# Splitting queries and keys into float32r parts at their projection instead of in the attention

## The chip, the cores and the metric

The kernel runs on one core of a Trainium2 chip. The metric is the device time in microseconds (us), the median of several runs. The engines are TensorE (PE, with its weight loads as PEld), VectorE (DVE), ScalarE (ACT), GpSimd (POOL) and SyncE (SP), which here issues the DMAs.

## The reference

One mixer layer on x of 2048 tokens and 1024 columns, all float32. A normalised input goes through one projection of 7168 columns; eight attention heads of 128 columns and four mLSTM heads use its parts; both results are gated, concatenated and projected back.

```python
h = rmsnorm(x, norm_g)
u = jnp.einsum("bsd,de->bse", h, w_in)                    # 1024 -> 7168
q_a, k_a, v_a, z_a, x_m, o_m, z_m = jnp.split(u, cuts, axis=-1)
for window, dilation in ((128, 1), (512, 4), (2048, 16)):
    o, l = dilated_window_attention(heads(q_a), heads(k_a), heads(v_a), window, dilation, slopes)
    ...
att = jnp.sum(wts[..., None] * jnp.stack(outs), axis=0) * silu(z_a)
...                                                       # conv, headwise linear, gates
hm = mlstm_chunkwise(q_m, k_m, v_m, log_i, log_f)         # then normalised per head, times silu(z_m)
x = x + jnp.einsum("bse,ed->bsd", concat([att, mls]), w_out)
return rmsnorm(x, final_g)
```

## The kernel before

**Precision.** A float32 operand is split into two float32r parts, hi (a rounded copy, ACT, L98) and lo (the rest, DVE, L99). A product is three matmuls: hi by hi, lo by hi, hi by lo.

**Projection (0 to about 1241 us).** There are 28 steps: two halves of the tokens (1024 each), and in each 14 steps for the kinds q, k, x, v, z, m, o, two steps each; the first are q0, q1, k0, k1. A step is seven products of a Strassen scheme, numbered 1 to 7; the operands of product m on the token side are the tiles h`m`h and h`m`l, on the weight side `whi` and `wlo`. Each product is 24 matmuls of 128x512 (L349) into PSUM tiles `pb` (two of them, for products 2, 1, 3 and 5; product 6 adds to the tile of 3) and `pa` (one, for 4; product 7 adds to it). `evac` adds them into the output tiles `o0` (one buffer) and `o1` (two) with ACT copies (L404) and DVE additions (L409, L411). After a step, `post` works on these tiles. For q and k it only stores them to `q_d` and `k_d` in DRAM; for the others it also applies a gate or the convolution.

**Background work.** `todo` is a list of generators, of which `run_post` takes one piece at each of four places in every product. Its first entry is `norm_later`: it normalises the second half's tokens in four blocks of two groups each. A group loads x into two `xc` tiles, squares them on ACT (L240, the output goes to `th` tiles), forms the inverse root on DVE (L243 to L94), scales (L247), transposes on PE (L252, four transposes of 128x128 at a time into the one PSUM tile `aux`), and copies with a factor on DVE (L255). Then each block makes seven Strassen operands (L262 on DVE, L265 on ACT; six of the seven combine or copy into `th` tiles) and stores them to `s_d` (L266). `scratch` gives tiles by tag: `xc` and `th` have two buffers each, and a tile is given out again only when everything that uses the earlier one is done.

**What sets the order.** Instructions are recorded in program order; a scheduler then fixes one order for each engine, and a piece of work that has to wait for a buffer of a tag stands behind the work that gives this buffer back.

**Attention and mLSTM (1241 to about 2109 us).** A head has 16 blocks, each twice (R=0, neighbouring keys; R=1, keys by residue of the token number), so 32 units; `attention` runs `qk` for one unit, `flip` for the unit two before, `pv` for the one three before, with the mLSTM and, later, the mLSTM half of the output projection (`early`) between them. `qk_split` (L617 on) prepares 512 tokens of a head: scaled hi and lo of q (ACT L620, DVE L621), both again in residue order (POOL L623, twice), and hi and lo of k (ACT L625, DVE L626). There are 32 such calls. `q_load` brings 256 KB, `k_load` 1 MB.

**Output projection (to 2217 us).** `early`, `att_tiles` and `load_wo` load raw 128x512 tiles (`wor`, `qh`) and split them into `me`, `we` and others (L98, L99); the matmuls are L1142 to L1144 and L1188 on.

Of the kernel before, what the change touches and what calls it, by code (L numbers as in the profile page):

```python
# [27 lines left out]
def kernel(  # L28
# [28 lines left out]
    q_d = dtile("q_d", [AH, 128, T])  # L57
    k_d = dtile("k_d", [AH, 128, T])
# [378 lines left out]

    def silu2(dst, th, src):
        nc.scalar.activation(th, src, AF.Tanh, scale=0.5)
        nc.vector.scalar_tensor_tensor(dst, th, 1.0, src, op0=ALU.add, op1=ALU.mult)  # L440

    def post(st, c):
# [14 lines left out]
        elif kind in "qkzm":  # L457
# [8 lines left out]
            dst = {"q": q_d, "k": k_d, "z": za_d}.get(kind)  # L466
            if kind == "m":
                for i in range(2):
                    nc.sync.dma_start(chunks(zm_d, e0 + i, hf * 8, 8), o[:, i, 3:].rearrange("p (c t) -> p c t", c=8))
            elif kind == "k":  # L470
                for i in range(2):
                    nc.sync.dma_start(residues(dst[e0 + i])[:, :, hf * 256:(hf + 1) * 256],
                                      o[:, i, 3:].rearrange("p (r q) -> p r q", r=4))
            else:
                nc.sync.dma_start(dst[e0:e0 + 2, :, tk].rearrange("e p t -> p e t"), o[:, :, 3:])
# [126 lines left out]

    def q_load(d, g):
# [11 lines left out]

    def qk_split(d, g):
        qr = d["qr", g] = by_r[-1]  # L617
        c = -1.0 / math.sqrt(128.0)
        hi, lo = qhi[:, g % 2], qt[:, g]
        nc.scalar.activation(hi, f(lo), AF.Copy, scale=c)  # L620
        nc.vector.scalar_tensor_tensor(lo, f(lo), c, f(hi), op0=ALU.mult, op1=ALU.subtract)  # L621
        for i, t in enumerate((hi, lo)):
            nc.gpsimd.tensor_copy(residues(qr[:, i, g % 2]), t.rearrange("p (j r) -> p r j", r=4))  # L623
        hi, lo = (residues(d[n])[:, :, g * 128:(g + 1) * 128] for n in ("kh", "k"))
        nc.scalar.activation(hi, f(lo), AF.Copy)  # L625
        nc.vector.tensor_tensor(lo, f(lo), f(hi), ALU.subtract)  # L626
# [39 lines left out]
    for i, (st, m) in enumerate(stream):  # L666
# [18 lines left out]
        if st == steps[-2] and m == ORDER[0]:  # L685
# [4 lines left out]
            qt = pre.tile([128, 4, 512], F32R, name="q")  # L690
            qhi = pre.tile([128, 2, 512], F32R, name="qh")
            first_load = k_load(pre, 0)
            for g in range(4):
                q_load(first_load, g)
# [27 lines left out]
    def qk(at, d, u):  # L722
        R, b = u
        g, r = b // 4, b % 4
        kh, kl, bl, st = d["kh"], d["k"], d["bl"], d["st"]
        ps = pq.tile([128, 512], F32, name="pq")
        if R:
# [3 lines left out]
            ks = lambda t: t[:, r * 512:r * 512 + n]  # L731
        else:
# [3 lines left out]
            ks = lambda t: t.rearrange("p (r b j) -> p b r j", r=4, b=16)[:, max(b - 1, 0):b + 1]  # L736
# [8 lines left out]
        qhr, qlr = (d["qr", g][:, i, g % 2] for i in range(2))  # L745
        qh, ql = (t[:, r * 128:(r + 1) * 128] for t in ((qhr, qlr) if R else (qhi[:, g % 2], qt[:, g])))
# [105 lines left out]
    def attention(at):  # L852
        qlag, slag = 0, 2
# [8 lines left out]
        for i in range(len(units) + 3):  # L862
            if i < len(units):
                h, u = units[i]
                if i == 0:
                    by_r.append(at.tile([128, 2, 2, 512], F32R, name="oL", bufs=2))
                    kh = at.tile([128, T], F32R, name="oR", bufs=2)
                    D_[0] = head_tiles(at, first_load)
                    D_[0]["kh"] = kh
                    qk_split(D_[0], 0)  # L870
                S_[i] = qk(at, D_[h], u)
# [7 lines left out]
            if i < len(units):  # L879
                h, (R, b) = units[i]  # L880
                if R and b % 4 == qlag and h + 1 < AH:
                    if b == qlag:
                        D_[h + 1] = k_load(at if h % 2 == 0 else pre, h + 1)
                    if b >= 4:
                        q_load(D_[h + 1], b // 4 - 1)
                if not R and b == qlag and h:
                    q_load(D_[h], 3)
# [174 lines left out]
    def raw_tile():  # L1062
        raws[0] += 1
        if raws[1] and raws[0] % 3 == 0:
            return pre.tile([128, 512], F32, name="qh")
        return woB.tile([128, 512], F32, name="wor", bufs=2)

    def att_tiles(b, i):
        if i == 0:
            pool, tag = ((pre, "q"), (ax[0], "qr"), (at, "kh"), (at, "k"))[mixes[0] % 4]  # L1070
            mixes[0] += 1
            MIX[b] = pool.tile([128, 2, 2, 4, 128], F32R, name=tag)
        t = MIX[b]
        raw = raw_tile().rearrange("p (e t) -> p e t", e=4)
        nc.sync.dma_start(raw, att_d[4 * i:4 * i + 4, :, b * 128:(b + 1) * 128].rearrange("e p t -> p e t"))
        split(t[:, i, 0], t[:, i, 1], raw)


    def load_wo(e):
# [3 lines left out]
        for n in range(2):  # L1083
            c = slice(n * 512, (n + 1) * 512)
            raw = raw_tile()
# [6 lines left out]
    def early():  # L1092
# [4 lines left out]
        def w_get(n, e):  # L1097
            raw["w", n, e] = woB.tile([128, 512], F32, name="wor", bufs=2)
            nc.sync.dma_start(raw["w", n, e], w_out[(KT + e) * 128:(KT + e + 1) * 128, n * 512:(n + 1) * 512])

        def w_split(n, e):
            t = W[n, e] = woB.tile([128, 2, 512], F32R, name=f"we{e}")
            split(t[:, 0], t[:, 1], raw.pop(("w", n, e)))
# [12 lines left out]

        seq = [(n, b) for n in range(2) for b in range(NB)]
        late = None
        w_get(0, 0)
        m_get(0, 0, 0)  # L1120
        w_split(0, 0)
        m_split(0, 0, 0)
        yield 0
        for e in range(1, 8):
            w_get(0, e)
            if e == 4:
                m_get(0, 0, 1)
                w_split(0, e)
                m_split(0, 0, 1)
            else:  # L1130
                w_split(0, e)
            if e % 2:
                yield 0
        for s, (n, b) in enumerate(seq):
# [4 lines left out]
            for e in range(8):  # L1139
# [9 lines left out]
                if swap:  # L1149
                    if e in (1, 2):  # L1150
                        w_get(1, e - 1)
# [3 lines left out]
                elif nxt:  # L1155
                    if e in (0, 3):
                        m_get(*nxt, e // 3)
                    if e == 4:
                        m_split(*nxt, 0)
# [3 lines left out]
            if swap:  # L1163
                for e in range(3, 8):
# [3 lines left out]
                    elif e < 8:  # L1168
                        m_get(*nxt, e - 6)
                    yield 0  # L1170
                m_split(*nxt, 0)
                m_split(*nxt, 1)
                yield 0
            elif nxt:
                m_split(*nxt, 1)
# [187 lines left out]
```

## Time and profile before

| | |
|---|---|
| Median of three runs | 2225.6 us (2224.17 to 2228.0) |
| The profiled execution, its own time | 2220.11 us |
| Its span (first to last instruction) | 2217.2 us |
| Mean granted TensorE clock | 0.988 |
| PE busy | 2126.7 us, 96% of the span |
| DVE, ACT, POOL busy | 1488.1, 942.8, 251.8 us |
| DMA read and written | 222.13 and 117.24 MB |

The page puts PE first: it is busy nearly always. The stages differ, though, so the table of windows, in which each row is a stage with every engine's busy time in it, is the one to read first. The list of waits says where an engine stood still and for what; the chain follows the work that ended last; the timeline gives single instructions with their start and duration. A matmul's busy time is longer than the spacing between two of them (0.39 us beside starts 0.23 us apart), since they overlap.

### The profile page before, as it was taken

What the parts mean: (1) busy time and instruction counts of PE and PEld (TensorE: products, weight loads), DVE (VectorE), ACT (ScalarE), POOL (GpSimd) and SP (SyncE); (2) the same over time, 40 slices, a digit from 0 to 9 for tenths busy, and PEclk for the clock granted to TensorE, in tenths of its full rate; (3) what the DMA queues carried; (4) which work ended last, traced back from release to release, by engine and by line L of the source; (5) the groups of instructions that cost most, each with busy time, mean ns of one, the idle gap of its engine ahead of it and who ended that gap; (6) DMA issues with size and microseconds to landing.
All of it is one profiled execution on the core that took longest, in us unless ns stands there. A gap on an engine that the chain in (4) does not pass through costs nothing.

```text
span 2217.2 us, 32676 instructions
## 1 busy us (share of the span) xinstructions
PE 2126.7 (96%) x11826; PEld 1788.0 (81%) x11826; DVE 1488.1 (67%) x3050; ACT 942.8 (43%) x1905; POOL 251.8 (11%) x221
## 2 busy tenths in 40 slices
PE   5999999999999999999999999999898999999998
PEld 4777888998878888787779888888887788777886
DVE  8887768556696558576666578868777644643654
ACT  6433333333383223334344555655555645532221
POOL 2200000000000000000000223343342221210000
PEclk9999999999999999999999999999999999999999
DMA  4256343432263333343324677776675664565442
GB/s 154 95 177 190 114 159 115 158 114 101 90 204 133 114 114 105 125 138 115 133 77 160 186 203 208 213 234 188 195 211 178 192 184 157 173 193 176 162 138 86
DMA packets 278896, 341.52 MB, mean 154 GB/s; under 512 B 22224, under 2 KB 194704, under 8 KB 276688
## 3 DMA queue, kind: packets, MB, share of 16 engines
q1 hardware_dynamic: 277872, 338.85, 48.2%
q8 instruction: 93, 1.52, 0.3%
q10 hardware_dynamic: 864, 0.59, 0.1%
q14 instruction: 67, 0.55, 0.1%
HBM read 222.13 MB, written 117.24 MB: 153 GB/s over the span
## 4 chain that ended last, share of the span: by engine, by line
PE 74%; DVE 9%; DMA 8%; issue 5%; ACT 3%; POOL 1%; SPq 0%; ACTq 0%; DVEq 0%; POOLq 0%
PE pb L349 31%; PE pa L349 12%; PE pm L780 3%; PE pu L997 2%; PE pt L762 2%; PE pu L985 2%; DMA wor<-mls_d 2%; DMA wor<-in_w_out 1%; DMA k<-k_d 1%; PE aux L500 1%; PE aux L510 1%; PE pq L748 1%; PE pq L750 1%; PE pq L749 1%; PE pu L982 1%
## 5 line engine op out<-in xcount | busy, mean ns | idle before, releaser
L98 ACT ACTIVATE whi<-ws 128x1024 fp32r<-128x1024 f32 x140 | 148.2, 1059 | 376.5 <-PE pb L349 209.4
L99 DVE TENSOR_TENSOR wlo<-ws,whi 128x1024 fp32r<-128x1024 f32 x140 | 171.8, 1227 | 81.3 <-ACT whi L98 80.4
L139 DVE TENSOR_TENSOR ws<-w,w 128x1024 f32<-128x1024 f32 x140 | 172.1, 1229 | 24.0 <-DMA w<-in_w_in 22.4
L754 ACT ACTIVATE s<-s,st 128x256 f32<-128x256 f32 (+3 forms) x256 | 134.9, 527 | 76.0 <-DVE st L752 68.8
L411 DVE TENSOR_TENSOR o<-pb,o 128x1024 f32<-128x1024 f32 x84 | 102.8, 1224 | 92.9 <-PE pb L349 91.9
L752 DVE CUSTOM_DVE_ANT_0 s<-pq,bl 128x256 f32<-128x256 f32 (+3 forms) x256 | 114.2, 448 | 43.3 <-PE pq L750 32.0
L612 POOL COPY bl<-bl 128x256 f32<-128x256 f32 x8 | 6.4, 796 | 1150.5 <-DMA q<-q_d 1111.3
L767 ACT ACTIVATE p<-pt 128x256 f32<-128x256 f32 (+1 forms) x192 | 81.3, 424 | 105.7 <-PE pt L762 104.6
L762 PE MATMUL pt<-sc,s 128*128 128x128 f32 x568 | 107.7, 279 | 7.1 <-ACT p L767 5.3
L98 ACT ACTIVATE whi<-w 128x1024 fp32r<-128x1024 f32 x56 | 59.2, 1057 | 125.2 <-PE pb L349 118.7
L1142 PE MATMUL pu<-we,me 128*128 128x512 f32 x256 | 106.6, 417 | 5.3 <-ACT me L98 4.4
L411 DVE TENSOR_TENSOR o<-pa,o 128x1024 f32<-128x1024 f32 x56 | 68.4, 1221 | 62.8 <-PE pa L349 62.8
L1143 PE MATMUL pu<-we,me 128*128 128x512 f32 x256 | 102.1, 399 | 2.9 <-DVE me L99 2.9
L1144 PE MATMUL pu<-we,me 128*128 128x512 f32 x256 | 101.2, 395 | 0.0
L780 PE MATMUL pm<-p,vc 128*128 128x128 f32 x640 | 96.3, 281 | 3.3 <-DVE p L765 1.7
L404 ACT ACTIVATE o<-pb 128x1024 f32<-128x1024 f32 x84 | 84.9, 1016 | 15.6 <-DVE o L411 9.8
L780 PEld LDWEIGHTS pm<-p,vc 128*128 128x128 f32 x640 | 84.0, 195 | 7.0 <-ACT p L767 3.5
L99 DVE TENSOR_TENSOR wlo<-w,whi 128x1024 fp32r<-128x1024 f32 x56 | 68.3, 1220 | 27.5 <-ACT whi L98 27.5
L762 PEld LDWEIGHTS pt<-sc,s 128*128 128x128 f32 x568 | 72.7, 143 | 17.3 <-ACT p L767 6.7
L99 DVE TENSOR_TENSOR me<-wor,me 128x512 fp32r<-128x512 f32 x64 | 48.4, 758 | 56.0 <-ACT me L98 55.9
L780 PE MATMUL pm<-p,vn 128*128 128x128 f32 x496 | 78.7, 279 | 5.1 <-ACT p L767 5.1
L997 PE MATMUL pu<-v,kw 128*128 128x257 f32 x240 | 71.6, 401 | 9.4 <-DVE C L1000 4.8
(592 smaller groups left out, 6565.9 us busy)
## 6 DMA issues: line engine op xcount, KB each, us to landing
w<-in_w_in SPq DMA_DIRECT2D x112, 512.0 KB
wor<-mls_d SPq DMA_DIRECT2D x64, 256.0 KB
q_d<-o SPq DMA_DIRECT2D x8, 1024.0 KB
k_d<-o SPq DMA_DIRECT2D x16, 512.0 KB
vm_d<-vm SPq DMA_DIRECT2D x32, 256.0 KB
xc_d<-xc SPq DMA_DIRECT2D x32, 256.0 KB
qm_d<-qm SPq DMA_DIRECT2D x32, 256.0 KB
v_d<-o SPq DMA_DIRECT2D x8, 1024.0 KB
```

The costliest lines, as they stand in the source:

```text
L98: nc.scalar.activation(hi, raw, AF.Copy)
L99: nc.vector.tensor_tensor(lo, raw, f(hi), ALU.subtract)
L139: eng.tensor_tensor(s, a, b, ALU.add if sign > 0 else ALU.subtract)
L349: nc.tensor.matmul(out, lhsT, rhs, start=start, stop=stop, skip_group_check=True)
L411: nc.vector.tensor_tensor(dst, ps, src, op)
L752: nc.vector.tensor_tensor_reduce(s[:, :n], ps[:, :n], bias, 1.0, 3e38, ALU.add, ALU.min, accum_out=st[:, col:col + 1])
L754: nc.scalar.activation(s[:, :n], s[:, :n], AF.Exp, bias=st[:, col:col + 1], scale=-1.0, accum_out=st[:, 16 + col:17 + col])
L762: nc.tensor.transpose(pp[:, i * 128:(i + 1) * 128], s[:, i * 128:(i + 1) * 128], ident)
L780: nc.tensor.matmul(od, v, p[:, j * 128:(j + 1) * 128], start=j == 0, stop=j == m - 1)
L997: nc.tensor.matmul(u[:, 0:257], kw[:, 2 * i + e, :], v[:, i], start=True, stop=True)
L1142: nc.tensor.matmul(acc, m[:, 0, j], w[:, 0], start=e == 0, stop=False)
L1143: nc.tensor.matmul(acc, m[:, 1, j], w[:, 0], start=False, stop=False)
```

## The change

In the projection, `post` no longer stores raw q and k. For every 128 x 512 part it calls `halves`, which makes hi (in an `xc` tile) and lo (in place in the output tile) and stores both; for q it also makes both again in residue order on ACT, in `th` tiles, and stores them. `q_d` grows fourfold and `k_d` twofold. In the attention `qk_split` is gone: `q_load` brings all four forms of 512 queries (1 MB) into one of two tiles, and the two parts of k are loaded by two DMAs of 1 MB (`k_load` and the one into `kh`); for the first eight blocks of head 0 hi of k comes as a quarter of that (`kh0`). In the output projection a raw tile of the mLSTM or attention result is loaded into the place of lo and split there, so that no `wor` tile is taken for it, and its load stands earlier.

```diff
+    def halves(kind, h, hf, g, raw):
+        hi = scratch("xc", 2).bitcast(F32R)
+        lo = raw.bitcast(F32R)
+        if kind == "q":
+            c = -1.0 / math.sqrt(128.0)
+            nc.scalar.activation(hi, raw, AF.Copy, scale=c)
+            nc.vector.scalar_tensor_tensor(lo, raw, c, f(hi), op0=ALU.mult, op1=ALU.subtract)
+            for n, t in enumerate((hi, lo)):
+                nc.sync.dma_start(q_d[h, 2 * hf + g][:, n], f(t))
+                rt = scratch("th", 2)
+                nc.scalar.activation(residues(rt), f(t).rearrange("p (j r) -> p r j", r=4), AF.Copy)
+                nc.sync.dma_start(q_d[h, 2 * hf + g][:, 2 + n], rt)
+                yield
+        else:
+            split(hi, lo, raw)
+            for n, t in enumerate((hi, lo)):
+                nc.sync.dma_start(residues(k_d[h, n])[:, 2 * g:2 * g + 2, hf * 256:(hf + 1) * 256],
+                                  f(t).rearrange("p (r q) -> p r q", r=2))
+            yield
...
+            elif kind == "z":
+                nc.sync.dma_start(za_d[e0:e0 + 2, :, tk].rearrange("e p t -> p e t"), o[:, :, 3:])
+            else:
                 for i in range(2):
+                    for g in range(2):
+                        yield from halves(kind, e0 + i, hf, g, o[:, i, 3 + g * 512:3 + (g + 1) * 512])
             yield
...
     def q_load(d, g):
-        nc.sync.dma_start(f(qt)[:, g], q_d[d["h"]][:, g * 512:(g + 1) * 512])
+        pool = (pre, ax[0] if ax else None)[g % 2]
+        d["q", g] = pool.tile([128, 4, 512], F32R, name="q") if pool else at.tile([128, 4, 512], F32R, name="oL", bufs=2)
+        nc.sync.dma_start(f(d["q", g]), q_d[d["h"], g])
...
-        nc.sync.dma_start(f(d["k"]), k_d[h])
+        nc.sync.dma_start(f(d["k"]), k_d[h, 1])
...
-    def qk_split(d, g):
...
                 if R and b == 11 and h + 1 < AH:
                     head_tiles(at, D_[h + 1])
-                    D_[h + 1]["kh"] = (at, ax[0])[h % 2].tile([128, T], F32R, name="kh")
-                if R and b % 4 == slag:
-                    if b < 12:
-                        qk_split(D_[h], b // 4 + 1)
-                    elif h + 1 < AH:
-                        qk_split(D_[h + 1], 0)
+                    kh = D_[h + 1]["kh"] = (at, ax[0])[h % 2].tile([128, T], F32R, name="kh")
+                    nc.sync.dma_start(f(kh), k_d[h + 1, 0])
+                if R and b % 4 == 1 and (h or b > 1):
+                    d, g = (D_[h], b // 4 + 1) if b < 12 else (D_.get(h + 1), 0)
+                    if d and g > (1 if h == 0 and d is D_[0] else -1):
+                        q_load(d, g)
...
+    def in_place(t):
+        split(t[:, 0], t[:, 1], f(t[:, 1]))
...
         def m_get(n, b, i):
-            raw["m", n, b, i] = woB.tile([128, 512], F32, name="wor", bufs=2)
-            nc.sync.dma_start(raw["m", n, b, i], mls_d[b, i])
-
-        def m_split(n, b, i):
             t = M[n, b, i] = woB.tile([128, 2, 4, 128], F32R, name="me", bufs=3)
-            split(t[:, 0], t[:, 1], raw.pop(("m", n, b, i)).rearrange("p (e t) -> p e t", e=4))
+            nc.sync.dma_start(f(t[:, 1]).rearrange("p e t -> p (e t)"), mls_d[b, i])
```

The number of matmuls does not change. How the change moves instructions is seen best in step q1, the second. On PE before, in products 7 of q1 and 2 of k0 (the numbers behind the names count tiles), two sets of `norm_later`'s transposes (L252, of four each) stand between the matmuls:

```order
L349 MATMUL pa_719<-h7h_493,whi_811 128x512
L349 MATMUL pa_719<-h7l_494,whi_811 128x512
L349 MATMUL pa_719<-h7h_493,wlo_812 128x512
L252 MATMUL aux_940<-sc_94,xc_903 128x128 x4
L349 MATMUL pa_719<-h7h_493,whi_811 128x512
L349 MATMUL pa_719<-h7l_494,whi_811 128x512
L349 MATMUL pa_719<-h7h_493,wlo_812 128x512
L349 MATMUL pb_1006<-h2h_194,whi_891 128x512
L252 MATMUL aux_953<-sc_94,xc_904 128x128 x4
L349 MATMUL pb_1006<-h2l_195,whi_891 128x512
```

On PE after, product 7 of q1 comes right behind product 3, and behind it stand the same two sets and all that follow, up to the last:

```order
L349 MATMUL pa_719<-h7h_493,wlo_812 128x512
L252 MATMUL aux_940<-sc_94,xc_903 128x128 x4
L252 MATMUL aux_953<-sc_94,xc_904 128x128 x4
L252 MATMUL aux_1084<-sc_94,xc_1040 128x128 x4
...
L252 MATMUL aux_1540<-sc_94,xc_1484 128x128 x4
L252 MATMUL aux_1590<-sc_94,xc_1553 128x128 x4
L252 MATMUL aux_1614<-sc_94,xc_1554 128x128 x4
L349 MATMUL pb_825<-h5h_606,whi_744 128x512
L349 MATMUL pb_825<-h5l_607,whi_744 128x512
```

Of the 64 transposes 56 (14 sets) now stand in one row without a product between them, and product 5 of q1 (`pb_825`) comes behind the last.

On ACT before, in the same step, the copy of product 1 out of PSUM (`o0_775<-pb_750`) stands among the rounding of weights (L98):

```order
L404 ACTIVATE o1_713<-pb_688 128x2x512
L98 ACTIVATE whi_744<-ws_746 128x1024
L98 ACTIVATE whi_779<-ws_781 128x1024
L404 ACTIVATE o0_775<-pb_750 128x2x512
L98 ACTIVATE whi_811<-ws_813 128x1024
L404 ACTIVATE o0_775<-pb_785 128x2x512
L98 ACTIVATE whi_891<-ws_893 128x1024
L240 ACTIVATE th_907,ss2_905<-xc_903 128x512
```

On ACT after, the same copy stands behind `norm_later`'s last pieces and behind `halves` of step q0 (L444 hi, L449 residue order; `o0_489` is the output tile of q0):

```order
L265 ACTIVATE th_1677<-gate_1619 128x512
L449 ACTIVATE th_1716<-xc_1712 128x512
...
L444 ACTIVATE xc_1846<-o1_341 128x512
L449 ACTIVATE th_1800<-o0_489 128x512
L404 ACTIVATE o0_775<-pb_750 128x2x512
L404 ACTIVATE o0_775<-pb_785 128x2x512
L449 ACTIVATE th_1827<-xc_1823 128x512
```

It was row 74 of ACT and is row 108: `o0` has one buffer, q0's `o0_489` is read until `th_1800`, and `halves` needs `xc` and `th` tiles, which come in turn behind all of `norm_later`. Product 5 takes the PSUM tile that this copy empties.

## Rows read from the trace of the kernel before

**Rows 1.** The page's head.
```profile
span 2217.2 us, 32676 instructions
```

**Rows 2.** Windows: start:end length, PE, PEld, DVE, ACT, POOL busy, PEclk, DMA share, GB/s.
```profile
106.00:235.00 129.00, 125.57 (x567) 99.56 (x566) 103.76 (x185) 42.61 (x62) 0.00 (x0) 1.00 0.57 181
235.00:1241.00 1006.00, 1005.94 (x5740) 849.04 (x5739) 669.06 (x720) 385.24 (x476) 0.65 (x1) 1.00 0.37 124
1241.00:1721.00 480.00, 444.46 (x2885) 395.91 (x2885) 365.64 (x1376) 280.65 (x850) 163.45 (x155) 0.96 0.71 209
1721.00:2109.00 388.00, 373.05 (x1886) 302.69 (x1886) 205.86 (x480) 158.65 (x383) 62.80 (x45) 1.00 0.56 177
2109.00:2217.00 108.00, 99.21 (x431) 80.46 (x429) 54.77 (x161) 20.34 (x53) 0.00 (x0) 0.97 0.33 110
```

**Rows 3.** The chain of waits, whole run: start us, us, what.
```profile
541.73 22.40 PE pb L349 x96
```

**Rows 4.** Timeline, PE in steps q1 and k1: start us, us, instruction, idle before.
```profile
106.42 0.39 PE L349 MATMUL pb<-h3h,wlo 128*128 128x512 f32 x1
106.65 0.39 PE L349 MATMUL pb<-h5h,whi 128*128 128x512 f32 x1
110.85 0.60 PE L252 MATMUL aux<-sc,xc 128*128 128x128 f32 x4
...
223.79 0.66 PE L252 MATMUL aux<-sc,xc 128*128 128x128 f32 x4
```

**Rows 5.** Timeline of one group of `norm_later`, all engines.
```profile
146.50 0.33 SPq L239 DMA_DIRECT2D xc<-in_x  x1
...
147.23 1.22 DVE L99 TENSOR_TENSOR wlo<-ws,whi 128x1024 fp32r<-128x1024 f32 x1
...
149.46 0.63 ACT L240 ACTIVATE th<-xc 128x512 f32<-128x512 f32 x1 [1.91 <-DMA xc<-in_x]
...
150.22 0.16 DVE L243 TENSOR_TENSOR ss<-ss 128x1 f32<-128x1 f32 x1 [0.51 <-ACT th L240]
```

**Rows 6.** Timeline of DVE in another group of `norm_later`.
```profile
172.79 0.16 DVE L243 TENSOR_TENSOR ss<-ss 128x1 f32<-128x1 f32 x1 [0.58 <-ACT th L240]
...
175.06 0.15 DVE L94 TENSOR_SCALAR rs_y<-rs_y 128x1 f32<-128x1 f32 x1
...
176.28 0.88 DVE L247 TENSOR_SCALAR xc<-xc,rs_y 128x512 f32<-128x512 f32 x2
177.51 0.69 DVE L255 TENSOR_TENSOR vm<-aux,ng 128x512 f32<-128x512 f32 x1 [0.34 <-PE aux L252]
```

**Rows 7.** The chain of waits from 100 to 240 us, the stores to `s_d`.
```profile
161.28 2.36 DMA s_d<-th
...
196.56 4.38 DMA s_d<-th
201.75 2.16 DMA s_d<-th
```

**Rows 8.** Waits in the attention and in `early`: who waits, for whom, us in total, times, longest.
```profile
PE pq L748 <- POOL oL L623: 1.5, 1, 1.5
...
ACT kh L625 <- DMA k<-k_d: 10.6, 4, 3.8
...
PE pu L1142 <- ACT me L98: 4.4, 3, 1.6
PE pu L1143 <- DVE me L99: 2.9, 6, 1.2
```

**Rows 9.** Windows, 7 us after the attention's start; columns as in Rows 2.
```profile
1245.00:1252.00 7.00, 6.23 (x29) 6.11 (x29) 3.69 (x17) 4.42 (x17) 3.73 (x4) 0.51 1.21 232
```

**Rows 10.** POOL's copies L623: their timeline beside DVE, and their sum in one window.
```profile
1573.86 1.10 POOL L623 CAST qr<-q 128x512 fp32r<-128x512 f32 x1 [0.76 <-DVE rs_y L86]
1574.04 0.94 DVE L92 TENSOR_TENSOR rs_t<-rs_t,sm 128x4 f32<-128x4 f32 x1
1575.83 0.16 DVE L92 TENSOR_TENSOR rs_t<-rs_t,sm 128x4 f32<-128x4 f32 x1
...
1241.00:1721.00 480.00, 65.09 (x240) 40.60 (x240) 0.00 (x0) 0.00 (x0) 48.05 (x43) 0.96 0.71 209
```

**Rows 11.** DMA: the queue's packets, MB, share of 16 engines; the issues for queries.
```profile
q1 hardware_dynamic: 277872, 338.85, 48.2%
...
q<-q_d SPq DMA_DIRECT2D x32, 256.0 KB
```

More of the change, by code (lines that the diff above doesn't have):

```diff
@@ L689 @@
             pre = prex.enter_context(tc.tile_pool(name="pre", bufs=1, side="right"))
-            qt = pre.tile([128, 4, 512], F32R, name="q")
-            qhi = pre.tile([128, 2, 512], F32R, name="qh")
+            kh0 = pre.tile([128, 1024], F32R, name="qh")
             first_load = k_load(pre, 0)
-            for g in range(4):
-                q_load(first_load, g)
+            q_load(first_load, 0)
+            nc.sync.dma_start(f(residues(kh0)), residues(k_d[0, 0])[:, :, 0:256])
     hx.close()
@@ L724, in qk @@
         g, r = b // 4, b % 4
-        kh, kl, bl, st = d["kh"], d["k"], d["bl"], d["st"]
+        kh, kl, bl, st = (residues(t) for t in (kh0 if d["h"] == 0 and b < 8 else d["kh"], d["k"])), None, d["bl"], d["st"]
+        kh, kl = kh
         ps = pq.tile([128, 512], F32, name="pq")
@@ L743, in keys @@
             return k
-        qhr, qlr = (d["qr", g][:, i, g % 2] for i in range(2))
-        qh, ql = (t[:, r * 128:(r + 1) * 128] for t in ((qhr, qlr) if R else (qhi[:, g % 2], qt[:, g])))
+        qh, ql = (d["q", g][:, 2 * R + i, r * 128:(r + 1) * 128] for i in range(2))
         w = max(n, 256)
@@ L865, in attention @@
                 if i == 0:
-                    by_r.append(at.tile([128, 2, 2, 512], F32R, name="oL", bufs=2))
+                    q_load(first_load, 1)
                     kh = at.tile([128, T], F32R, name="oR", bufs=2)
+                    nc.sync.dma_start(f(kh), k_d[0, 0])
                     D_[0] = head_tiles(at, first_load)
                     D_[0]["kh"] = kh
-                    qk_split(D_[0], 0)
+                h, u = units[i]
                 S_[i] = qk(at, D_[h], u)
@@ L1060, in mlstm, with att_get @@
             yield
[L1062 to L1066, printed above, removed]
+    def in_place(t):
+        split(t[:, 0], t[:, 1], f(t[:, 1]))
+    def att_get(b):
+        pool, tag = ((pre, "q"), (ax[0], "q"), (at, "kh"), (at, "k"))[b % 4]
+        MIX[b] = pool.tile([128, 2, 2, 4, 128], F32R, name=tag)
     def att_tiles(b, i):
         if i == 0:
[L1070 to L1076, printed above, removed]
+            att_get(b)
+        t = MIX[b][:, i]
+        nc.sync.dma_start(f(t[:, 1]), att_d[4 * i:4 * i + 4, :, b * 128:(b + 1) * 128].rearrange("e p t -> p e t"))
+        in_place(t)
     def load_wo(e):
@@ L1084, in load_wo @@
             c = slice(n * 512, (n + 1) * 512)
-            raw = raw_tile()
+            raw = woB.tile([128, 512], F32, name="wor", bufs=2)
             nc.sync.dma_start(raw, w_out[e * 128:(e + 1) * 128, c])
@@ L1115, in x_get, with w_split @@
             nc.sync.dma_start(raw["x", n, b], x[b * 128:(b + 1) * 128, n * 512:(n + 1) * 512])
+        def w_split(n, e):
+            t = woB.tile([128, 2, 512], F32R, name=f"we{e}")
+            split(t[:, 0], t[:, 1], W[n, e])
+            W[n, e] = t
         seq = [(n, b) for n in range(2) for b in range(NB)]
         late = None
[L1119 to L1132, printed above, removed]
+        for e in range(10):
+            if e >= 2:
+                w_split(0, e - 2)
+            if e < 8:
+                w_get(0, e)
+            if e % 4 == 3:
+                m_get(0, 0, e // 4)
                 yield 0
+        in_place(M[0, 0, 0])
+        in_place(M[0, 0, 1])
         for s, (n, b) in enumerate(seq):
@@ L1154, in early @@
                         w_get(1, e - 3)
[L1155 to L1159, printed above, removed]
+                if nxt:
+                    if e in (0, 2):
+                        m_get(*nxt, e // 2)
+                    if e in (4, 6):
+                        in_place(M[(*nxt, e // 2 - 2)])
             xr = raw.pop(("x", n, b))
@@ L1250 @@
     ax.append(ctx.enter_context(tc.tile_pool(name="ax", bufs=1)))
-    by_r.append(ax[0].tile([128, 2, 2, 512], F32R, name="qr"))
     with tc.tile_pool(name="mp", bufs=1) as mp:
```

61 lines of the change are left out of this document (13 added, 48 removed).

## The prediction

> **What bounds the kernel now.** I read the windows by stage first, then the chain, then the timeline of step q1, where the order changes, and last the waits of the attention. The windows show that the projection is TensorE from end to end: PE is busy 1005.94 of 1006 us there [rows 2], and one product after the other stands in the chain, four in 22.40 us, so 5.60 us each [rows 3]. Between 106 and 235 us `norm_later` runs beside it, and PE loses no more than 129 - 125.57 = 3.4 us [rows 2]. So whatever the change removes from DVE, ACT or POOL gains nothing in the projection, and whatever stops PE there is lost in full. In the attention (1241 to 1721) PE is idle for 480 - 444.46 = 35.5 us, and its mean granted clock is 0.96, which costs up to 0.04 x 480 = 19 us. From 1721 to 2109 it is idle for 15 us, at the end for 9 us [rows 2]. All that a lighter attention and output projection could give back is therefore 35.5 + 19 + 15 + 9 = 78 us at the very most.
>
> **Step q1: the new wait.** In the order of after, 14 sets of transposes of `norm_later` stand in one piece on PE, behind products 3 and 7 of q1 and ahead of product 5. Product 5 needs the PSUM tile that ACT's copy into `o0_775` empties; that copy now stands behind `th_1800`, the last of the residue copies that read `o0_489`; and these need `xc` and `th` tiles, which come behind all of `norm_later`. Queued behind the waiting matmul is everything that PE has left. Ahead of it on PE there are only transposes, so for this stretch the pace of `norm_later` by itself is the pace of the kernel. I sum it from the rows.
>
> Product 3 of q1 ends at 106.65 [rows 4]; with four sets of transposes (0.60 each, about 0.44 of it not overlapped) and product 7 (5.6) PE has done its matmuls at 106.65 + 5.6 + 4 x 0.44 = about 114. The first block's first group is transposed by about 109.
>
> One block, undisturbed, from the end of its first group's transposes to the same point of the next block:
> - its second group: load of x and two squares 150.22 - 146.50 = 3.7 [rows 5]; inverse root 175.06 + 0.15 - 172.79 = 2.4; scaling, two sets of transposes with the copy between them 2.6 (half of 0.88, then 0.60 + 0.69 + 0.60 and the hand-overs) [rows 4, 6]. Together 8.7.
> - its operands and the next block's first group: six operands go through two `th` tiles, the next squares need a `th` tile too, so three stores to `s_d` have to land one after the other. With r for one store and 0.7 for the operand ahead of it (the 0.69 of a DVE pass over 512 columns [rows 6]) this is 0.7 + 3 x (r + 0.7) + 0.8 for the squares [rows 5] + 2.4 + 2.6 = 8.6 + 3r.
>
> So a block takes 17.3 + 3r. The stores on the chain took 2.16 to 4.38 us [rows 7]. The queues are emptier in a stretch in which no weights are loaded, so I take r = 2.5 and get 25 us per block (24 with the shortest, 30.5 with the longest). The first block also has three operand builds of the weights left over on DVE, 3 x 1.22 [rows 5]. Its first group's point is 109, the fourth block's is 109 + 3.6 + 3 x 25 = 187.6, its second group is transposed at 196.3. Behind that come the last operands and the first halves of q, 14 `th` tiles up to `th_1800`, two at a time: six further trips of about 2.5 + 0.95 = 3.45, so 217. The copy (about 1 us) and the hand-over to PE bring product 5 to 219. PE thus stands from 114 to 219, 105 us, in which it does 14 sets of transposes (14 x 0.6 = 8.4) that it did in any case. **The stall is 97 us**; with r = 2.16 it is 91, with r = 4.4 about 125. Before, the first transposes began at 110.85 and the last at 223.79 [rows 4], beside the products: 113 us for four blocks. If `norm_later` kept that pace, with the halves of q behind it, the stall would be some 130 us.
>
> **The rest of the projection.** 32 q halves each bring three ACT passes and a DVE pass; the DVE passes are those taken out of the attention. ACT is busy 385 of 1006 us [rows 2], so the 128 additional passes (some 0.63 each, 80 us) fit as work. But the residue copies pass in order through two `th` tiles at about (0.63 + 0.9 + 2.5) / 2 = 2 us each, 16 in a step, 32 us, and the rounding of the weights stands between them; a step is 7 x 5.6 = 39.2 us, so this fits with little to spare. I take +3 in the first half and +3 in the second (0 to 8 each). When PE comes back after a rest its granted clock may be at the lower of its two levels, 1.2 GHz: after the pause at the attention's start it was 0.51 for 7 us [rows 9], 3.5 us lost. I take +4. The micro-waits beside `norm_later` go (-3). Together **+7 us**, between 0 and +25.
>
> **The attention and the output projection.** Gone are 64 POOL copies of 1.1 us, and 64 ACT and 64 DVE passes. None of these engines is the bound there (DVE 366, ACT 281, POOL 163 of 480 us), so only waits count. At the entry PE waits for POOL's L623 (1.5) and again behind it, about 3.5 us with DVE's and ACT's share, and 3.5 us of low clock follow [rows 8, 9]: 7. ACT stands 10.6 us before `kh` for the load of k, and its copies for other heads, for which PE then waits, stand behind it [rows 8]: 10. `me` in place and loaded earlier takes 4.4 + 2.9 [rows 8] and a little more: 8. That is **-25 us**. The bounds are -78 (all idle time and all lost clock) and +15: the k load is still there, and now PE itself would wait for it; the queue moves 64 MB more (q 8 to 32 MB, k 8 to 16 MB, both written and read), in proportion to 338.85 MB in 48.2% of the span [rows 11] about 200 us of 16 engines' time, half of it in the attention, whose share of 0.71 [rows 2] goes to about 0.85; at a head's end three loads of 1 MB come together, and a load that is 2 us late at each of seven heads costs 14.
>
> There is a row that speaks for more gain. While POOL's L623 ran for 1.10 us, a DVE pass of 128x4 took 0.94 us; 0.8 us after it, the same pass took 0.16 [rows 10]. The Trainium skill, page "SBUF — State Buffer", section "Who interferes with whom", says that DVE and GpSimd share one port pair, and that the lock on it is exclusive. By that rule the 43 copies of the window, 48.05 us [rows 10], could hold DVE for up to as long; the sum with all of this given back would be some 23 us lower. The trace agrees with the rule in single places only, so I leave it out of the sum, which goes by the waits of PE.
>
> **The sum.** The profiled execution has a span of 2217.2 us [rows 1]. 2217.2 + 97 + 7 - 25 = 2296.2; its own time was 2.9 us more than its span, and the median of the runs 5.5 us more than that: 2304.6, rounded to **2304 us**.
>
> **The rivals.**
> 1. *The stall comes, and the attention gives nothing back.* The 64 MB more fill the queues; PE waits for k and q where ACT did. For it: the share of 0.71 and the k loads that ACT waits for already. Against it: q has a step of some four units' lead and two tiles. 2304 + 25 to 40: about 2335.
> 2. *`norm_later` keeps the pace it had beside the products.* Its 113 us for four blocks may be due to the DRAM round trips, not to the products between. Stall 130 instead of 97: about 2337.
> 3. *The attention gives back nearly all its idle time.* For it: rows 10, and that POOL and ACT lose a third of their work. -70 instead of -25: about 2259.
> 4. *Faster.* The stall would have to be cheaper than the gain. The place is the reuse of the `th` tiles: if a store's landing isn't waited for (r near zero), a block takes 17.3, the six trips 5.7, and the stall shrinks by 3 x 7.5 + 15 to about 60; with the whole bound of 78 the time is 2225.6 + 60 + 7 - 78 = 2215. Between the 60 at r = 0 and the 91 at r = 2.16 the stall grows by 15 per us, so with the full gain faster begins below r of about 0.8. The shortest row is 2.16 [rows 7], which speaks against it.
> 5. *The change doesn't do what it says.* The moved instructions are in the order of each engine, and the stall hangs on two positions there, not on a timing; no chance of its own.
>
> **How the numbers follow.** Forecast 0.55; rival 1 0.17; rival 2 0.13; rival 3 0.11; rival 4 0.03; the last 0.01 for a balance near nothing. The forecast by itself holds 2280 to 2325 (r from 2.16 to 3.5, the attention from -40 to -5). The range reaches over rivals 1 and 2 above and to rival 3 below: 2256 to 2350. A measurement of this kernel can tell 0.2%, 4.5 us, from no change. Faster by more than that 0.03, within it 0.01, slower 0.96.
>
> **What would show it.** In the profile after, PE should be nearly idle from about 114 to 219 us, with transposes alone, ended by a wait of product 5 for ACT L404; the blocks of transposes should stand 25 us apart. The last matmul of the projection should come about 100 us later than at 1241. From there to the end it should take about 950 us instead of 976, with DMA share near 0.85 in the attention and no wait of PE for POOL. It would be wrong if PE found products to do inside that stretch, if the blocks stood closer than 20 us, or if PE waited for loads of k or q at each head.

## The result and the profile after

The changed kernel took 2340.99 us (median of 4 runs, 2338.21 to 2342.08) against 2224.89 for the kernel before: a ratio of 1.0524, 95% interval 1.0498 to 1.055, so 116 us slower. The profiled execution has a span of 2339.8 us. The forecast was 2304, the range 2256 to 2350: the direction and most of the loss came as forecast, and one term, a gain behind the projection, did not come.

Where the time went is told by two rows of the timeline and the two spans. The last matmul of the projection started at 1241.43 before and at 1356.90 after; from there to the end it took 975.8 us before and 982.9 after. So the projection lost 115.5 us, and the rest lost 7.1 where I had expected a gain of 25. The profiled execution of the kernel before was 5 us faster than its median (2220.11 beside 2224.89), that of after 1 us slower, so the 7.1 are not certain: by the medians the whole change costs 116 us, which is the loss in the projection alone. That the gain did not come is clear either way.

The page of after, its head, and in 40 slices the granted clock and the DMAs (compare [rows 1]):

```profile
span 2339.8 us, 33080 instructions
...
PEclk9955999999999999999999999999999999999999
DMA  4235752344235486444332487877978677655442
```

Timeline of PE, the last matmul of the projection, in the kernel before and in after:

```profile
1241.43 0.28 PE L349 MATMUL pa<-wlo,h7h 128*128 128x256 f32 x1
```
```profile
1356.90 0.28 PE L349 MATMUL pa<-wlo,h7h 128*128 128x256 f32 x1
```

Windows of after (columns as in [rows 2]): step q1 and what follows, and the attention, shifted so that it starts with the attention:

```profile
106.00:235.00 129.00, 33.91 (x131) 24.24 (x131) 58.09 (x143) 35.34 (x57) 0.00 (x0) 0.58 0.47 148
...
1357.00:1837.00 480.00, 439.22 (x2844) 389.16 (x2842) 323.18 (x1311) 253.59 (x791) 102.83 (x104) 0.96 0.81 256
```

PE worked 33.91 us in the window in which it had worked 125.57 [rows 2], at a mean granted clock of 0.58. In the attention DVE, ACT and POOL all have less to do (366 to 323, 281 to 254, 163 to 103 us), and PE did no more for it: 439 against 444 us. The DMA share went from 0.71 to 0.81. The timeline of PE in the pause (the bracket is the idle time before, and what ended it; the first four rows are the second set of transposes of the first group of each block):

```profile
110.33 0.60 PE L252 MATMUL aux<-sc,xc 128*128 128x128 f32 x4
...
139.55 1.12 PE L252 MATMUL aux<-sc,xc 128*128 128x128 f32 x4 [0.78 <-DVE vm L255]
...
165.41 1.12 PE L252 MATMUL aux<-sc,xc 128*128 128x128 f32 x4 [0.78 <-DVE vm L255]
...
191.13 1.11 PE L252 MATMUL aux<-sc,xc 128*128 128x128 f32 x4 [0.79 <-DVE vm L255]
...
201.25 1.12 PE L252 MATMUL aux<-sc,xc 128*128 128x128 f32 x4 [0.78 <-DVE y L255]
226.31 0.79 PE L349 MATMUL pb<-h5h,whi 128*128 128x512 f32 x1 [23.95 <-ACT o L404]
```

The pause ends at 226.31 with product 5 of q1, released by the copy L404, as the order had it. The chain between the last transposes and that copy shows the two `th` tiles going round: six stores of about 2.4 us, one after the other, three of `norm_later` and three of the halves:

```profile
204.38 2.47 DMA s_d<-th
...
207.58 2.33 DMA s_d<-th
...
210.75 2.28 DMA s_d<-th
...
213.14 1.12 ACT th L449
...
214.28 2.50 DMA q_d<-th
...
217.94 2.46 DMA q_d<-th
...
221.56 2.51 DMA q_d<-th
...
225.23 0.12 ACT o L404
```

The list of PE's waits, whole run, has the pause in its first two rows. Of the waits in the attention the longest is now one for a load, and another load stands third (the last two rows here). In the kernel before, a load of `xc` cost PE 0.9 us, all loads behind the projection 2.5, and its waits there named ACT, DVE and POOL above all [rows 8].

```profile
PE aux L252 <- DVE xc L247: 64.9, 7, 12.8
PE pb L349 <- ACT o L404: 27.9, 3, 23.9
...
PE pt L968 <- DMA xc<-xc_d: 8.5, 4, 5.3
...
PE pm L791 <- DMA vn<-v_d: 6.0, 1, 6.0
```

### The profile page after: what moved, and what is told of

The parts are those of the page before. It is cut to its first block, busy times and chain, and to the rows that moved or that the text cites. A ratio compares the mean times of both kernels' runs of the same rounds, so it can differ in the third digit from the quotient of the medians.

```text
span 2339.8 us, 33080 instructions
## 1 busy us (share of the span) xinstructions
PE 2145.2 (92%) x11826; PEld 1797.8 (77%) x11826; DVE 1481.9 (63%) x3050; ACT 1019.8 (44%) x1969; POOL 176.6 (8%) x157
## 4 chain that ended last, share of the span: by engine, by line
PE 74%; DMA 10%; DVE 7%; ACT 4%; issue 2%; SPq 2%; POOL 1%; POOLq 0%; ACTq 0%; DVEq 0%
PE pb L349 30%; PE pa L349 12%; PE pm L791 4%; PE pu L1003 2%; PE pu L991 2%; PE pt L773 2%; DMA q_d<-th 2%; DMA me<-mls_d 2%; ACT th L449 1%; DMA wor<-in_w_out 1%; PE aux L530 1%; PE pu L988 1%; PE pu L1138 1%; PE aux L520 1%; PE pq L759 1%
## 5 line engine op out<-in xcount | busy, mean ns | idle before, releaser
L98 ACT ACTIVATE whi<-ws 128x1024 fp32r<-128x1024 f32 x140 | 148.1, 1058 | 317.7 <-PE pb L349 177.0
L98 ACT ACTIVATE whi<-w 128x1024 fp32r<-128x1024 f32 x56 | 59.2, 1056 | 112.1 <-PE pb L349 106.9
L759 PE MATMUL pq<-kh,q 128*128 128x256 f32 x224 | 91.0, 406 | 2.1 <-DVE st L763 2.1
L349 PE MATMUL pb<-h5h,whi 128*128 128x512 f32 x160 | 66.5, 416 | 27.9 <-ACT o L404 27.9
L404 ACT ACTIVATE o<-pb 128x1024 f32<-128x1024 f32 x84 | 84.8, 1016 | 12.3 <-DVE o L411 8.0
```

The costliest lines, as they stand in the source:

```text
L98: nc.scalar.activation(hi, raw, AF.Copy)
L349: nc.tensor.matmul(out, lhsT, rhs, start=start, stop=stop, skip_group_check=True)
L759: nc.tensor.matmul(ps[:, 0:w], qh, keys(kh), start=True, stop=False)
```

## The experiments

Two questions: is the pause due to the tiles that `norm_later` holds, and where did the attention's gain go?

**norm_later behind step v1 (e1_late_norm), and the same edit in the kernel before (b1_late_norm).**

```diff
-    todo = [norm_later()]
+    todo = []
...
             todo += [post(st, 0), post(st, 1)]
+            if i == 55:
+                todo.append(norm_later())
```

> The changed kernel, with norm_later put into the list of background work only behind step v1 (the eighth), so that it no longer holds the xc and th tiles while the halves of q and k are made. Theory A (the loss is the pause of PE in step q1, because the halves wait for tiles that norm_later holds): the pause of 92 us without a product and the 3 us behind it go, the last matmul of the projection comes at 1241 to 1248 us instead of 1357, and the time is 2226 to 2234 us; what is left against the kernel before is the attention (its part of the span was 983 us against 976). Rival B (the 128 additional ACT passes and the 32 MB of stores cost the projection time by themselves, wherever norm_later stands): the pause only moves, and the time stays above 2300 us.

> The kernel before, with norm_later put behind step v1 in the same way: the control for the run above. Theory A: norm_later costs the projection no more than 3 to 4 us where it stands, so moving it gives 2219 to 2226 us. Rival B: it costs as much or more beside the steps of v, o and z as it did beside q and k (2226 to 2235 us); then a part of what the run above shows is due to the new place and not to the halves.

e1_late_norm took 2243.45 us, ratio 1.0071 (1.005 to 1.0092); b1_late_norm 2232.78, ratio 1.0037 (1.002 to 1.0054). The windows of e1_late_norm, first where the pause was, then where `norm_later` now runs:

```profile
106.00:235.00 129.00, 128.92 (x554) 103.39 (x552) 89.97 (x94) 75.44 (x85) 0.00 (x0) 1.00 0.67 223
407.00:579.00 172.00, 161.73 (x1011) 141.29 (x1010) 129.52 (x217) 66.19 (x92) 0.00 (x0) 1.00 0.52 165
```

With the halves of q and k in it, and without `norm_later`, the stretch from the end of q1 into step x0 is all TensorE: 128.92 of 129 us, more than in the kernel before. The pause is gone, and with it 0.0453 of 2225, 101 us. So the halves cost the projection next to nothing by themselves; they cost it when they run beside `norm_later`. What stays is another price: the last matmul of the projection starts at 1251.91, mostly because `norm_later` leaves PE idle for 10 us in its new place, where 3.4 were lost in the old [rows 2]. In the control, without any halves, it starts at 1251.12, so less than 1 us is due to the halves. Theory A holds for the pause, though its 1241 to 1248 and its 2226 to 2234 us were missed by this price; rival B of the control holds for the place.

**Another order of steps (w1_order).** The first half begins with o and v, whose `post` needs no `xc` or `th`, and `norm_later` runs beside these.

```diff
-    steps = [(0, *s) for s in kinds[:8] + kinds[12:] + kinds[8:12]] + [(1, *s) for s in kinds]
+    steps = [(0, *s) for s in kinds[12:] + [("v", 0), ("v", 1)] + kinds[:4] + [("x", 0), ("x", 1)] + kinds[8:12]] + [(1, *s) for s in kinds]
```

> The changed kernel with another order of steps in the first half: o0, o1, v0, v1 first, whose post takes no xc or th tiles, then q0, q1, k0, k1, x0, x1, z, m. norm_later stays first in the list and so runs beside o1, v0 and v1. Theory A (the pause comes from the tiles alone, and the new place of norm_later cost e1_late_norm 10 us): the projection ends near 1241 us, and the time is 2228 to 2238 us, slower than before by the attention alone. Rival B (the halves cost the steps of q and k something even with norm_later gone): above 2240 us.

2236.03 us, ratio 1.0076 (1.0059 to 1.0093). The time is in theory A's range, but the last matmul of the projection starts at 1251.89, again 10 us late and not near 1241. Its windows, beside `norm_later` and later:

```profile
106.00:235.00 129.00, 124.06 (x971) 119.00 (x970) 101.44 (x179) 45.55 (x65) 0.00 (x0) 1.00 0.58 180
400.00:579.00 179.00, 174.98 (x794) 127.78 (x793) 131.45 (x158) 65.79 (x91) 0.00 (x0) 1.00 0.41 129
```

Beside `norm_later` PE is idle for 4.9 us, only 1.5 more than in the kernel before. Another 4.0 lie between 549 and 568 us, where neither `norm_later` nor the halves of q and k run, and 1.0 between 300 and 400, beside the halves, in waits for L404; the rest of the 10 us was not traced. Two orders without a pause thus give about the same time, 0.7 to 0.8% over the kernel before, and in both the projection takes some 10 us more, though PE is idle in different places. Why was not tried.

**The changed kernel without residue copies (a2_no_th).**

```diff
-                rt = scratch("th", 2)
-                nc.scalar.activation(residues(rt), f(t).rearrange("p (j r) -> p r j", r=4), AF.Copy)
-                nc.sync.dma_start(q_d[h, 2 * hf + g][:, 2 + n], rt)
+                nc.sync.dma_start(q_d[h, 2 * hf + g][:, 2 + n], f(t))
```

> The changed kernel without the residue copies of q on ACT: the parts are stored twice as they are, so the bytes and the number of DMAs stay, and the halves of q need no th tiles. norm_later stands where it stood. Theory A (the pause is the time of norm_later alone, 201 us for its last transposes, and behind it the th tiles two at a time, which took till 226): PE still stands while norm_later runs, but goes on at about 212 instead of 226, and the time is 2325 to 2332 us. Rival B (the tail is due to the stores or the xc tiles, not to th): 2338 to 2343 us.

2335.34 us, ratio 1.0482 (1.0455 to 1.0508). Its timeline of PE at the end of the pause, and two stores from its chain there:

```profile
198.09 1.12 PE L252 MATMUL aux<-sc,xc 128*128 128x128 f32 x4 [0.78 <-DVE y L255]
218.17 0.80 PE L349 MATMUL pb<-h5h,whi 128*128 128x512 f32 x1 [18.96 <-ACT o L404]
```
```profile
202.83 3.54 DMA q_d<-xc
...
212.58 4.44 DMA q_d<-o
```

PE still stands through all of `norm_later`, and goes on 19 us behind its last transposes instead of 24. So leaving out the `th` tiles of the halves saves 5 of these 24 us, not 14: neither theory's number. The chain shows what stands behind them: stores of the halves from the `xc` tile and from the output tile, for which the next half and the copy L404 wait. As the second store of each part reads the same tile here, the run adds a use of these tiles while it takes away that of `th`. The `th` tiles are thus not the only ones through which the halves hold up that copy.

No run gave the halves tiles of their own. That the pause needs `norm_later` and the halves side by side is shown by e1_late_norm and w1_order; that the tiles are the link is read from the order and from the chain.

**No split in the attention (b2_no_split).** In the kernel before, `qk_split` does nothing, and raw q and k stand in for the parts: the split and the residue order are left out.

> The kernel before with the split of q and k left out of the attention: raw q and raw k are used in place of hi, lo and the residue order, and nothing takes the place of the 64 passes of ACT, 64 of DVE and 64 copies of POOL; loads and matmuls are as before. It is the most that taking the split out of the attention can give. Theory A (the expected 17 us of attention gain are there, and the 64 MB more of DMA take them back): 2195 to 2212 us. Rival B (they were hidden; PE waits in the attention for the chain of softmax and mLSTM, not for the split): 2218 to 2226 us.

2206.14 us, ratio 0.9911 (0.9892 to 0.993): 20 us faster. Theory A: as a sum, my 17 us for the attention were there to be had.

**Small loads (e2_small_loads).** e1_late_norm with one form of q and one part of k loaded and used for all.

```diff
-        nc.sync.dma_start(f(d["q", g]), q_d[d["h"], g])
+        nc.sync.dma_start(f(d["q", g])[:, 0], q_d[d["h"], g][:, 0])
...
-                    nc.sync.dma_start(f(kh), k_d[h + 1, 0])
```

> The kernel of e1_late_norm (norm_later behind step v1), of which the attention loads only as much of q and k as the kernel before: one of the four forms of q (256 KB instead of 1 MB) and one part of k, used in place of all forms; the stores, the matmuls and the rest stay. Without the split and without its replacement by loads: theory A (the attention's gain of about 20 us, which b2_no_split showed, is taken back by the 32 MB more of loads, with PE waiting for vn, xc and nb behind them in the queue): 2215 to 2226 us, some 20 to 27 us under e1_late_norm's 2243, and PE's waits for DMA xc and vn (10.9 and 6.9 us there) are gone. Rival B (the loads are hidden; the attention is slower for another reason, its order on PE or the loads' places): 2238 to 2246 us.

2214.71 us, ratio 0.9974 (0.9961 to 0.9986), against 1.0071 for e1_late_norm: 0.0097 x 2225 = 22 us. The stores of all forms are still made. Its window of the attention and that of e1_late_norm (each from its start):

```profile
1250.00:1730.00 480.00, 448.55 (x2917) 399.52 (x2916) 326.42 (x1333) 259.17 (x810) 107.58 (x108) 0.96 0.72 214
```
```profile
1252.00:1732.00 480.00, 439.35 (x2847) 388.89 (x2846) 323.95 (x1316) 253.71 (x791) 102.69 (x104) 0.96 0.82 256
```

With the DMA share at 0.72 PE does 2917 matmuls in the window instead of 2847. The two longest waits of PE for loads in e1_late_norm's attention are these; a third, for `nb`, has 2.1 us. In e2_small_loads the one for `vn` is 4.0, and the others are gone:

```profile
PE pt L970 <- DMA xc<-xc_d: 10.9, 5, 4.3
PE pm L793 <- DMA vn<-v_d: 6.9, 1, 6.9
```

Theory A: the loads take the gain back.

**The output projection alone (b3_in_place).** The kernel before with `in_place`, `att_get` and the new `m_get` and `w_get` of the change.

> The kernel before with the change to the output projection alone: raw tiles of the mLSTM and attention result are loaded into the place of lo and split there, m_get stands earlier. Theory A (my term of 8 us: PE waits 4.4 and 2.9 us for ACT and DVE on me): 2216 to 2221 us. Rival B (hidden, or given back to the attention's units that run beside it): 2223 to 2229 us.

2215.64 us beside 2220.33, ratio 0.9985 (0.9971 to 0.9999). A gain of some 3 us (by the interval 0 to 6), not of 8.

**Fewer bytes (w2_strided), and another order of loads at the entry (w3_entry).** w2_strided is w1_order without residue copies; PE takes every fourth column of q as weights for R=1.

```diff
-        qh, ql = (d["q", g][:, 2 * R + i, r * 128:(r + 1) * 128] for i in range(2))
+        qh, ql = (d["q", g][:, i].rearrange("p (j r) -> p r j", r=4)[:, r] if R else
+                  d["q", g][:, i, r * 128:(r + 1) * 128] for i in range(2))
```

> The kernel of w1_order without the residue copies of q: the projection stores hi and lo once (64 ACT passes and 64 stores fewer), the attention loads 512 KB of q instead of 1 MB, and the units with R=1 take every fourth column of q as weights for PE. If loads are what takes the attention's gain back (theory A): 8 to 20 us under w1_order, 2210 to 2228 us, so that it would beat the kernel before. Rival B (reading every fourth column makes the weight loads slow, or the loads are not the cause): the same as w1_order or slower.

> The kernel of w2_strided with the loads of vn, vc and zs of head 0 issued ahead of the second q load and the k hi load at the entry of the attention. Theory A (PE's wait for vn, 3.9 us there, comes from their place in the queue): 3 to 6 us under w2_strided's 2226, about 2221. Rival B (the queue is full there, and PE waits for q or k instead): 2224 to 2228 us.

w2_strided: 2225.77 us, ratio 1.0027 (1.0012 to 1.0041), 11 us under w1_order, as theory A said, though its weight loads are dearer; the kernel before it did not beat. PE's waits for `xc` and `vn` fell from 11.1 and 7.4 us to 4.6 and 3.9. The groups by line of the attention, in w1_order and in w2_strided (busy us, mean ns of one, idle before):

```profile
L760 PEld LDWEIGHTS pq<-k,q 128*128 128x128 f32 x160 | 30.6, 191 | 2.6
```
```profile
L758 PEld LDWEIGHTS pq<-k,q 128*128 128x128 f32 x162 | 42.1, 260 | 1.7 <-issue 0.2
```

w3_entry: 2233.4 beside 2227.3, ratio 1.0025 (1.0009 to 1.0041), the same. The wait moved, as rival B said; PE's waits in its attention and in that of w2_strided:

```profile
PE pq L757 <- DMA oL<-q_d: 3.1, 1, 3.1
```
```profile
PE pm L789 <- DMA vn<-v_d: 3.9, 1, 3.9
```

**POOL's copies (b4_no_copies, b5_strided, b6_copies_act).** The kernel before without them; b3_in_place with strided weights in their place; b3_in_place with the copies on ACT:

```diff
-            nc.gpsimd.tensor_copy(residues(qr[:, i, g % 2]), t.rearrange("p (j r) -> p r j", r=4))
+            nc.scalar.activation(residues(qr[:, i, g % 2]), f(t).rearrange("p (j r) -> p r j", r=4), AF.Copy)
```

> The kernel before without the 64 residue copies on POOL alone (the splits on ACT and DVE stay; the units with R=1 read the parts in natural order, so nothing is added). It parts the 20 us of b2_no_split. Theory A (the copies hold DVE up through a port that POOL and DVE share, as the DVE pass of 0.94 us beside a copy suggested, and this is the larger part): 12 to 20 us under the kernel before. Rival B (the copies are hidden, the gain is that of the 64 ACT and 64 DVE passes): 0 to 6 us under it.

> The kernel of b3_in_place in which the units with R=1 take every fourth column of q as weights, as in w2_strided, so that POOL's copies go without any load or pass in their place. In w2_strided these weight loads took 308 ns instead of 190, and the first matmul behind them 467 instead of 367, so up to 0.1 us x 384 loads of R=1 = 38 us of PE time, of which part is hidden. Theory A (w2_strided gained net of this, so it costs under 10 us): 2205 to 2216 us, faster than both kernels. Rival B (the price of the strided loads is as large as the copies' gain): 2216 to 2226 us.

> The kernel of b3_in_place with the 64 residue copies made in the attention by ACT instead of POOL: the same copies as the change puts into the projection, left where they were, with no more bytes to load. b4_no_copies gained 10 us by leaving POOL's copies out, b3_in_place 3 us by its own edit; ACT would have 64 x 0.63 = 40 us more work in a stage in which it is busy 281 of 480 us. Theory A (the copies cost as they are POOL's, by what they do to DVE and by their 1.1 us each, and ACT has room): 2212 to 2220 us against 2225 for the kernel before, faster than both kernels. Rival B (ACT's passes now stand ahead of the p that PE waits for, 9.6 us already in b4_no_copies): 2221 to 2230 us.

b4_no_copies: 2217.69 beside 2227.3, ratio 0.9954 (0.9937 to 0.9971), 10 us, half of what b2_no_split gave and just between the theories. Its window of the attention:

```profile
1241.00:1721.00 480.00, 447.75 (x2902) 397.48 (x2902) 353.83 (x1382) 284.11 (x856) 109.70 (x107) 0.96 0.73 210
```

DVE is busy 353.83 us with 1382 instructions, where it was 365.64 with 1376 [rows 2]. It does about the same work in 12 us less once 43 copies with 48 us of POOL are gone. Passes that read PSUM kept their time (L752 for 128x256: 417 and 418 ns on average), while the one over `hm`, whose tiles all lie in SBUF, got shorter, here the same line in the kernel before and in b4_no_copies:

```profile
L1031 DVE TENSOR_SCALAR hm<-hm,sm 128x256 f32<-128x256 f32 x64 | 29.3, 499 | 0.5
```
```profile
L1028 DVE TENSOR_SCALAR hm<-hm,sm 128x256 f32<-128x256 f32 x64 | 26.2, 455 | 0.5
```

That agrees with the rule of the Trainium skill, page "SBUF — State Buffer", section "Who interferes with whom", that DVE and GpSimd share one port pair and that the lock on it is exclusive; here the copies cost DVE a quarter of their own time.

b5_strided: 2227.36, ratio 0.9999 (0.9983 to 1.0015). Rival B: the slow weight loads cost as much as leaving the copies out gave. b6_copies_act: 2223.8 beside 2228.15, ratio 0.9981 (0.9962 to 1.0), 4 us, at the edge of rival B's range. PE's waits for ACT's p are 13.1 and 5.0 us there, where they were 4.6 and 3.6, and one copy took ACT as long as POOL:

```profile
PE pm L780 <- ACT p L767: 13.1, 8, 4.8
PE pt L762 <- ACT p L767: 5.0, 4, 2.4
```
```profile
L623 ACT ACTIVATE qr<-qh x29: 1103/1139/1170, 1268.1 to 1907.0; 128x512 fp32r<-128x512 f32 x29
```

b3_in_place and b6_copies_act are the fastest that leave nothing out, 0.15 and 0.19% under the kernel before, with intervals that end at it; none is clearly faster.

## Why the prediction was right, and where it was wrong

**The pause.** Its place and its size were right. I had PE standing from 114 to 219; its last matmul of product 7 started at 116.16, and product 5 at 226.31. I had the first group's transposes of the blocks 28.6, 25 and 25 us apart; they are 29.2, 25.9 and 25.7 apart (110.33, 139.55, 165.41, 191.13). The stores to `s_d` on the chain, which I took at 2.5, took 2.28 to 2.81, and the tail had the six trips that I counted. Inside a block the working was right only in its sum. I had three stores land one after the other; the chain shows two in each block, here in the first:

```profile
127.02 2.62 DMA s_d<-th
...
130.45 2.30 DMA s_d<-th
```

What the third store would have taken went to the transposes, which ran at the low clock (1.09 to 1.12 us a set instead of 0.60, 2 us in a block), and to passes that I had taken too short. That a block came out so near to 25 us is in part luck. The 7 us that I was early: the first group came 2 us later, the blocks took 4 us longer together, and the tail 1.

**The rest of the projection.** My +7 was too little: 115.5 in all against 97 + 7 = 104. Behind the pause PE waits 3.05 more at 264.78 for L404, with residue copies ahead of that copy on ACT, and 0.93 at 863.88 in the second half, where I took 3 each. The clock is at its lower level from 226.3 to 229.8 and again behind that wait, to 270.8:

```profile
226.00:230.00 4.00, 3.69 (x9) 2.97 (x10) 0.69 (x1) 3.84 (x5) 0.00 (x0) 0.53 0.46 164
230.00:235.00 5.00, 5.00 (x23) 4.00 (x23) 1.93 (x3) 3.58 (x4) 0.00 (x0) 1.00 0.81 282
265.00:270.00 5.00, 5.00 (x12) 3.92 (x13) 1.05 (x1) 3.57 (x4) 0.00 (x0) 0.50 0.96 282
...
264.78 0.80 PE L349 MATMUL pb<-h5h,whi 128*128 128x512 f32 x1 [3.05 <-ACT o L404]
```

Matmuls start 0.43 us apart there instead of 0.23, which costs 1.7 + 2.8 = 4.5 us; I took 4. The stall itself is 226.3 - 116.4 = 110 less the 8.4 of transposes, 101.5 where I had 97. That makes 101.5 + 3 + 1 + 4.5 = 110. Of the 5.5 us left, 2.7 are PE's waits at 397 to 402 us (L520, L542), and some 2 lie ahead of 106 us, where PE is busy for 76.27 us instead of 78.51; profiled executions differ there by as much (77.75 in a2_no_th).

**The attention and the output projection.** This step failed. I put -25 into the sum; the stretch from the projection's end took 7 us more in the profiles, and by the medians about as long as before. The gain was there as a sum: 20 us for the split (b2_no_split) and 3 for the output (b3_in_place) make 23. Its parts were not as I told them: 10 of the 20 go with POOL's copies alone (b4_no_copies), for which I had counted only the waits at the entry, and the output gave 3 instead of 8. What failed is that I left the loads out of the sum. I had raised the DMA share from 0.71 to about 0.85 (0.81 came) and had named +15 as a bound, but counted nothing for it. The loads cost 22 us (e1_late_norm against e2_small_loads; by the two intervals together some 16 to 27). They do not delay PE by q and k, which I looked at: no wait of PE for either stands in the list of after. PE waits for `xc` of the mLSTM, for `vn` and for `nb`, 10.9 + 6.9 + 2.1 = 19.9 us in e1_late_norm's attention against 4.0 in e2_small_loads. `vn`, for one, is issued behind two loads of 1 MB, of q and of k. Rival 1, at about 2335, is what happened, though not by the waits for k and q that it names; I gave it 0.17. The 2341 lie above the 2280 to 2325 that the forecast held by itself.

**From the span to the median.** The sum added 2.9 + 5.5 = 8.4 us, as in the kernel before. After has 1.2 (2340.99 - 2339.8), so here the sum was 7 us too high, which by luck hid a part of the miss.

**The port.** Rows 10 pointed at more than I counted, the 10 us of b4_no_copies. As the loads took the gain back, it did not change the outcome.

**The other rivals.** Rival 2 (the old pace of 113 us for four blocks) is out, as the spacing shows: they took 92. Rival 3 is out, as nothing was given back. Rival 4 needed stores of 0.8 us; they took 2.28 at least.

## What to carry to other kernels

Moving work into a stage in which its engines have room can still stop the bottleneck, if the moved work takes the scratch tiles of a long background task: look in the order for the one buffer that the next matmul waits for, and sum the background task by itself. Work that is done once and stored in more forms is paid in loads; price them by every transfer that shares the queue, not by the engine that reads them. And size a gain by leaving the work out altogether: two runs (b2_no_split, e2_small_loads) parted a gain and a loss that the total hid.

## What the runs showed of the hardware

A pass of ACT over 128x512 that reads every fourth element and writes them in a row took 1.13 us, where a plain one (L444) took 0.63; on POOL the same copy took 1.12 in the median, in the kernel before. All copies L449 of after in two groups, L444 of after, and one group of POOL's L623 of before (ns, least/median/most):

```profile
L449 ACT ACTIVATE th<-xc x32: 1107/1127/1145, 210.9 to 875.0; 128x512 f32<-128x512 f32 x32
L449 ACT ACTIVATE th<-o x32: 1111/1130/1144, 213.1 to 877.2; 128x512 f32<-128x512 f32 x32
L444 ACT ACTIVATE xc<-o x32: 615/629/636, 200.5 to 867.4; 128x512 fp32r<-128x512 f32 x32
```
```profile
L623 POOL CAST qr<-qh x29: 1086/1120/1646, 1261.5 to 1893.2; 128x512 fp32r<-128x512 f32 x29
```

So ACT is no faster than POOL at this copy. Weight loads of PE with every fourth column in half of them took 260 ns on average instead of 191 (w2_strided beside w1_order; in its timeline 310 to 330 ns for the strided ones and 190 for the others), and what they cost was as large as the gain from dropping POOL's copies (b5_strided).
